# The opening of a hybrid trunk kernel and the step between its two passes, rewritten: stationary modulation blocks, other row statistics, input put in tile by tile

## The chip, the cores and the metric

One core of a Trainium2 chip runs the whole program. The metric is device time in microseconds, lower is better. PE is the matrix engine, PEld its weight loads, DVE the vector engine, ACT the scalar engine, POOL the third one, and SP issues nearly all DMAs from one queue in order.

## The reference, cut to what matters

One layer over 2048 latent tokens and 256 context tokens of width 1024, in float32. The token mixer is a bidirectional RG-LRU, a SwiGLU FFN follows. Both sub-layers begin with an RMS norm whose scale and shift come from a vector `c` (latent) or `c_ctx` (context):

```python
mx = split(silu(c) @ mod_w + mod_b, 6); mc = split(silu(c_ctx) @ mod_w + mod_b, 6)
hx = rms_norm(x, norm_mix_g) * (1 + mx[1]) + mx[0]       # 2048 tokens
hc = rms_norm(ctx, norm_mix_g) * (1 + mc[1]) + mc[0]     # 256 tokens
yx = rglru_mixer(hc, hx, ...)     # conv, gates, scans both ways, context first
x = x + mx[2] * yx
x = x + mx[5] * swiglu(modulate(rms_norm(x, norm_ffn_g), mx[3], mx[4]), ...)
```

So mx[0], mx[1], mc[0], mc[1] and the norm's row statistics (one 1/rms per token) have to stand before the first projection of the mixer, and the other four parts of mx not before the end of the mixer.

## The kernel before

Activations lie transposed: 128 channels on the partitions, tokens along the row; 1024 channels are eight tiles k. A float32 product is made of three float32r matmuls: `parts` (L83, L84) splits an operand into a rounded part (ACT copy) and its rest (DVE subtract), and `mm3` (L106 to L108) adds high by high, high by low and low by high. `norm` here means: a column of 1/rms values (`rstd_of`, fifteen small DVE instructions), spread over the partitions by a matmul of ones with a diagonal (`spread`, L138 and L142), copied out of PSUM by ACT.

**Sweep 1** covers the mixer's projections. The latent tokens stand in two halves s = 0 and s = 1 of 1024 tokens (two columns of 512 each), called the two passes here. Each pass runs over the ten 128-wide channel blocks n of the recurrence; m counts the 20 blocks. For each block `rec_unit` projects (48 matmuls of 512 columns; in pass 0 also 24 of 258 columns for the context), `conv` and `conv_parts` make the short convolution and split it, `gate_unit` projects the gate (48 matmuls of 512), `z_unit` makes the two gates of both directions (24 of 512; in pass 0 also 12 of 256 for the context), and `scan_exp`, `scan_root`, `scan_context`, `scan` finish the previous block. On PE, ACT and DVE the instructions of `blocks` stand in the order of the program text; SP's order is made by a scheduler. Weights come through `fetch`: a load into a buffer `raw` (4 of them), the split into a buffer `op` (6). Other buffers: `w` (9 rows of 1024), `hc` (4, the context's input), `hx` (8, the input of the pass at hand, so pass 1 takes over the buffers of pass 0), and four PSUM pairs of two banks.

**The opening** is everything ahead of the first `rec`. `first_loads` loads the context and the first 512 tokens; `mod_first` and four times `mod_quarter` make the scale A and shift B: the modulation weights are the moving operand, split like the others, 16 matmuls of 512 columns a quarter, with a stationary block that holds silu(c) and silu(c_ctx) in four columns; the result is turned back into a column by four narrow matmuls with `sel` (L256). `first_stats` squares all input tiles on ACT and sums over the channels with narrow matmuls (each tile's squares the stationary operand, one column of ones the moving one, L331): 56 for the context and the first 512 tokens, 32 for the second 512. `first_scale`, `first_apply` multiply by 1/rms, apply A and B and split. The order of the opening on all engines is the scheduler's. All of pass 0's input is ready before the first `rec`.

**The step between the passes** stands around blocks m = 8 and 9. `norm1_stats` has gathered sums of squares of the 1024 tokens of pass 1 from token-major rows (m = 0 to 7), `norm1_row` spreads 1/rms at m = 8, and then both remaining gates of pass 0 are projected, because they read `hx` for the last time; `norm1_apply` loads a tile of x (L379), scales it on DVE (L382), adds the shift and rounds on ACT (L383) and takes the rest on DVE (L384), for four tiles ahead of z(8), two ahead of z(9) and two behind it; rec(10) follows. The modulation's other 32 rows (`mod_rest`) are dot products on DVE, three for each block from m = 0 on.

Sweep 2 (the output projection and the FFN) starts when sweep 1 is done and isn't touched.

Of the kernel before, what the change touches and what calls it, by code (L numbers as in the profile page):

```python
# [44 lines left out]
class Trunk:  # L45
# [107 lines left out]
    def constants(self, first):  # L153
        nc, cp, io = self.nc, self.cp, self.io
# [4 lines left out]

        def load(key, shape):  # L160
            t = cp.tile(list(shape), F32, name=f"c_{key}")
            nc.sync.dma_start(t, io[key])
            return t

        cc = load("cc", (P, KD, 2))
        first()
        self.mod_b = load("mod_b", (P, 48))
        self.g_mix = load("g_mix", (P, KD))
        self.g_ffn = load("g_ffn", (P, KD))
# [5 lines left out]
    def constants_rest(self):  # L175
        nc, cp, io = self.nc, self.cp, self.io

        def load(key, shape):
            t = cp.tile(list(shape), F32, name=f"c_{key}")
            nc.sync.dma_start(t, io[key])  # L180
            return t

        self.conv_w = load("conv_w", (P, NB, 4))
        self.conv_b = load("conv_b", (P, NB))
        self.gate_b = load("gate_b", (P, 2, 2, NB))
        lam = load("lam", (P, 2 * NB))
        self.lam = lam
        self.state = cp.tile([P, 2, NB], F32, name="state")
        self.halo = cp.tile([P, NB, 4], F32, name="halo")

    def decay(self):
# [6 lines left out]
        self.behind(v.tensor_scalar(out=m, in0=lam, scalar1=-1.0, scalar2=0.0, op0=ALU.mult, op1=ALU.max),  # L198
                    self.scale_done)
        self.behind(v.tensor_scalar(out=e, in0=lam, scalar1=-1.0, scalar2=None, op0=ALU.mult), self.scale_done)  # L200
# [17 lines left out]
    def mod_first(self):  # L218

        nc = self.nc
        self.A = self.cp.tile([P, KD, 2], F32, name="A_mix")
        self.B = self.cp.tile([P, KD, 2], F32, name="B_mix")
        z = self.wp.tile([P, KD, P], F32, tag="raw", name="mod_z", bufs=RAWS)
        nc.gpsimd.memset(z, 0.0)
        st = self.wp.tile([P, KD, P], F32R, tag="op", name="mod_st", bufs=OPS)
        nc.vector.tensor_copy(z[:, :, 0:2], self.sc)  # L230
        nc.vector.tensor_copy(st, z)
        nc.vector.tensor_tensor(out=st[:, :, 2:4], in0=self.sc, in1=st[:, :, 0:2].bitcast(F32), op=ALU.subtract)
        sel = self.cp.tile([P, 2], F32, name="sel")
        nc.vector.tensor_tensor(out=sel, in0=self.ident[:, 0:2], in1=self.ident[:, 2:4], op=ALU.add)
        self.mod_st, self.sel = st, sel
        self.sc_row = self.te.tile([P, D], F32, tag="row", name="silu_row", bufs=1)
        for q in range(2):
            row = self.spread(self.sc[:, 4 * q : 4 * q + 4, 0], f"silu{q}")
            nc.vector.tensor_copy(self.sc_row[:, q * C : (q + 1) * C], row)

    def mod_quarter(self, q):
        nc, st, sel = self.nc, self.mod_st, self.sel
        ps = self.bank(f"ps_mod{q}")
        for j in range(KD // 2):
            raw = self.raw(self.io["mod_f"][q, j], f"modf{q}_{j}")
            self.last_mod = self.last_raw
            hl = self.parts(raw, f"modf{q}_{j}")
            for k in (2 * j, 2 * j + 1):
                for w in range(2):
                    nc.tensor.matmul(ps, st[:, k, :], hl[:, w, (k % 2) * C : (k % 2 + 1) * C],  # L250
                                     start=(k == w == 0), stop=(k == KD - 1 and w == 1))
# [37 lines left out]

    def norm1_stats(self, j):


        nc = self.nc
# [794 lines left out]
```

## Time and profile before

| | |
|---|---|
| three runs | 2366.94, 2371.41, 2372.65 us; median 2371.41 us |
| the profiled execution | 2367.48 us, of which the trace spans 2365.7 us |
| PE busy | 2236.8 us, 95% of the span |
| DVE, ACT busy | 1510.9 us (64%), 1170.9 us (49%) |
| mean granted clock of PE | 0.969 |

Matmuls are pipelined: a row's duration is longer than the distance to the next one, so distances of starts are used for rates. The granted clock is a share of 2.4 GHz; 0.5 is the lower of its two levels, 1.2 GHz. A line in brackets at the end of a row tells how long the engine was idle before it, and what ended that. Times of the trace are counted from the span's start.

### The profile page before, as it was taken

Reading aid. Unit: us, or ns where it says so; the run is one execution under the profiler, and the core shown is the slowest. Engines: PE = TensorE matmul, PEld = TensorE weight load, DVE = VectorE, ACT = ScalarE, POOL = GpSimd, SP = SyncE. Lnnn points to the kernel's source line nnn. Section 1 sums busy time; section 2 is a strip of 40 time slices with the busy share of each in tenths; the row PEclk is TensorE's granted clock in tenths of the full one; section 3 lists DMA queues with packets and bytes.
Section 4 is the critical chain, followed back from the end, with each engine's and each line's share of the span. In section 5 each row is a group of like instructions: output and inputs, shape, how many; then the busy total and the mean of one; then the engine's idle time right before and its main releaser. Section 6 shows DMA issues by size and latency. Waiting matters only on the chain.

```text
span 2365.7 us, 25944 instructions
## 1 busy us (share of the span) xinstructions
PE 2236.8 (95%) x9854; PEld 1844.2 (78%) x9854; DVE 1510.9 (64%) x1949; ACT 1170.9 (49%) x1416; POOL 1.6 (0%) x7
## 2 busy tenths in 40 slices
PE   7799997499999967999999999999999999999999
PEld 6688885388887855787877888878888888888887
DVE  5867776578888668767676555874555555545443
ACT  4467774577888325656564443453333333333332
POOL 0000000000000000000000000000000000000000
PEclk9699998799999988999999999999999999999999
DMA  6145453422123742444444476786522222246664
GB/s 227 64 160 178 169 178 112 164 80 67 63 74 105 276 143 89 143 151 142 152 144 145 161 238 221 219 289 229 188 81 81 80 80 81 80 134 211 226 220 144
DMA packets 127133, 354.14 MB, mean 150 GB/s; under 512 B 15136, under 2 KB 15136, under 8 KB 127008
## 3 DMA queue, kind: packets, MB, share of 16 engines
q1 hardware_dynamic: 127008, 352.48, 44.2%
q8 instruction: 77, 1.26, 0.2%
q14 instruction: 48, 0.39, 0.1%
HBM read 281.12 MB, written 71.30 MB: 149 GB/s over the span
## 4 chain that ended last, share of the span: by engine, by line
PE 67%; ACT 7%; DVE 4%; issue 2%; DMA 1%; DVEq 0%; ACTq 0%; SPq 0%
PE ps_dn L107 6%; PE ps_dn L108 6%; PE ps_dn L106 6%; PE ps_be L106 6%; PE ps_be L107 6%; PE ps_be L108 6%; PE ps_ep L108 3%; PE ps_wo L106 3%; PE ps_ep L107 3%; PE ps_wo L108 3%; PE ps_ep L106 3%; PE ps_wo L107 3%; ACT L77 2%; PE ps_rec L106 2%; PE ps_rec L107 2%
## 5 line engine op out<-in xcount | busy, mean ns | idle before, releaser
L107 PE MATMUL ps_dn<-op_xd,op_wd 128*128 128x512 f32 x704 | 274.2, 390 | 2.8 <-DVE op_xd L84 2.8
L108 PE MATMUL ps_dn<-op_xd,op_wd 128*128 128x512 f32 x704 | 273.9, 389 | 0.0
L106 PE MATMUL ps_dn<-op_xd,op_wd 128*128 128x512 f32 x704 | 269.9, 390 | 0.0
L84 DVE TENSOR_TENSOR op_wd<-raw_wd,op_wd 128x1024 fp32r<-128x1024 f32 x88 | 107.8, 1225 | 197.5 <-ACT op_wd L83 197.5
L83 ACT CAST op_wd<-raw_wd 128x1024 fp32r<-128x1024 f32 x88 | 92.7, 1054 | 265.9 <-PE ps_dn L108 214.6
L923 DVE TENSOR_TENSOR s<-ps_ep,s 128x512 f32<-128x512 f32 x88 | 60.7, 689 | 153.8 <-ACT s L948 114.6
L107 PEld LDWEIGHTS ps_dn<-op_xd,op_wd 128*128 128x128 f32 x704 | 132.1, 188 | 31.3 <-DVE op_xd L84 4.1
L106 PEld LDWEIGHTS ps_dn<-op_xd,op_wd 128*128 128x128 f32 x704 | 132.1, 188 | 28.0 <-ACT op_xd L83 0.4
L108 PEld LDWEIGHTS ps_dn<-op_xd,op_wd 128*128 128x128 f32 x704 | 132.1, 188 | 27.6
L106 PE MATMUL ps_be<-T,op_b 128*128 128x512 f32 x352 | 139.5, 396 | 9.5 <-ACT s L948 9.5
L77 ACT ACT_TABLE_LOAD x113 | 145.0, 1283 | 2.7 <-PEq L1082 0.7
L106 PE MATMUL ps_ep<-T,op_s 128*128 128x512 f32 x352 | 137.6, 393 | 8.3 <-ACT T L863 8.3
L108 PE MATMUL ps_be<-T,op_b 128*128 128x512 f32 x352 | 138.3, 393 | 0.0
L107 PE MATMUL ps_be<-T,op_b 128*128 128x512 f32 x352 | 138.3, 393 | 0.0
L108 PE MATMUL ps_ep<-T,op_s 128*128 128x512 f32 x352 | 137.4, 390 | 0.0
L107 PE MATMUL ps_ep<-T,op_s 128*128 128x512 f32 x352 | 137.2, 390 | 0.0
L106 PE MATMUL ps_rec<-hx,op_r 128*128 128x512 f32 x320 | 127.4, 398 | 7.5 <-ACT op_r L83 7.5
L948 ACT COPY s<-ps_be 128x512 f32<-128x512 f32 x44 | 25.7, 584 | 207.8 <-PE ps_be L108 207.8
L430 DVE SCALAR_TENSOR_TENSOR u<-ps_rec,c_conv_w,u 128x1024 f32<-128x1024 f32 x60 | 77.1, 1285 | 80.3 <-ACT u L427 78.8
L106 PE MATMUL ps_wo<-op_xo,op_wo 128*128 128x512 f32 x320 | 124.2, 393 | 2.6 <-ACT r L77 2.6
L107 PE MATMUL ps_rec<-hx,op_r 128*128 128x512 f32 x320 | 126.3, 395 | 0.2 <-DVE hx L357 0.2
L108 PE MATMUL ps_rec<-hx,op_r 128*128 128x512 f32 x320 | 126.1, 394 | 0.2 <-DVE op_r L84 0.2
(250 smaller groups left out, 5409.2 us busy)
## 6 DMA issues: line engine op xcount, KB each, us to landing
raw_wd<-in_down SPq DMA_DIRECT2D x88, 512.0 KB, 3.6
raw_xd<-d_act SPq DMA_DIRECT2D x88, 512.0 KB, 4.6
raw_ga<-in_gu SPq DMA_DIRECT2D x44, 512.0 KB, 3.9
raw_gb<-in_gu SPq DMA_DIRECT2D x44, 512.0 KB, 4.1
d_act<-s SPq DMA_DIRECT2D x88, 256.0 KB, 3.5
raw_xo<-d_rg SPq DMA_DIRECT2D x40, 512.0 KB, 4.2
raw_mod<-in_mod_t SPq DMA_DIRECT2D x32, 512.0 KB, 3.6
x<-in_x_t SPq DMA_DIRECT2D x48, 256.0 KB, 5.4
```

The source lines that it names most:

```text
L77: return self.table(self.nc.scalar.activation(out, in_, func, bias=bias, scale=scale))
L83: nc.scalar.copy(t[:, 0, :], raw)
L84: nc.vector.tensor_tensor(out=t[:, 1, :], in0=raw, in1=t[:, 0, :].bitcast(F32), op=ALU.subtract)
L106: ins = mm(ps, w[0], x[0], start=first, stop=False, skip_group_check=shared)
L107: mm(ps, w[0], x[1], start=False, stop=False, skip_group_check=shared)
L108: mm(ps, w[1], x[0], start=False, stop=last, skip_group_check=shared)
L430: v.scalar_tensor_tensor(out=part, in0=ps, scalar=cw[:, i : i + 1], in1=part, op0=ALU.mult, op1=ALU.add)
L923: v.tensor_tensor(out=t, in0=ps, in1=t, op=ALU.add)
L948: nc.scalar.copy(s3, be)
```

## The change

- **Modulation.** The weights are no longer split and no longer moving: each quarter is loaded as two tiles of 1 MB (`mod_load`), and `mod_half` takes each 128x128 block of it as the stationary operand, in float32, with the two columns silu(c), silu(c_ctx) as the moving one: 32 matmuls a quarter, 128 in all, into columns, so that no turning back is needed. Before, a float32 matmul of this kind appears in the trace as two instructions (two loads, two multiplications).
- **Statistics.** For the context and the first 512 tokens ACT squares and DVE adds over the tiles (`column_stats`), and seven narrow matmuls sum over the partitions; for the second 512 tokens the squares are summed along token-major rows on ACT (`token_stats`).
- **Input.** `apply` puts in a tile at a time: scale by A and 1/rms on DVE, shift and round on ACT, rest on DVE. The context's two extra columns are treated apart (`context_extra`).
- **Order.** The opening (`begin`) also stands in the order of the text on PE, ACT and DVE. Block 0's projections are taken into it and interleaved with the input: first half of rec and gate, context, second half of rec and gate. The decay constants are made at the start. `mod_rest` goes two and two for each block, none at m = 8, so that it is done before the step between the passes.
- **The step** (`turn`): the four first tiles of x are loaded into the `hc` buffers as soon as the context's input is no longer read, the diagonal is made at the head of m = 8, the spread follows rec(9) at once, and all eight tiles are put in behind the projection of gate(9); z(8), z(9) and rec(10) follow. `gate_unit` is cut into the projection and `gate_out` (the copy out of PSUM).

`mod_first`, `mod_quarter`, `norm1_stats`, `first_loads`, `first_stats`, `first_scale`, `first_apply`, `norm1_row` and `norm1_apply` go. The new code, with the unchanged and the removed lines left out where they tell nothing:

```diff
...
+    def mod_load(self, q):
+        ts = []
+        for half in range(2):
+            t = self.wp.tile([P, KD // 2, C], F32, tag="op", name=f"modf{q}_{half}", bufs=OPS)
+            self.nc.sync.dma_start(t, self.io["mod_f"][q, half])
+            ts.append(t)
+        return ts
+    def mod_half(self, ps, t, half):
+        for kk in range(KD // 2):
+            k = half * (KD // 2) + kk
+            for i in range(4):
+                self.nc.tensor.matmul(ps[:, i, :], t[:, kk, i * P : (i + 1) * P], self.sc[:, k, :],
+                                      start=(k == i == 0), stop=(k == KD - 1 and i == 3), skip_group_check=True)
...
+    def token_stats(self, t0, j, n, name):
+        nc = self.nc
+        xt = self.wp.tile([P, D], F32, tag="raw", name=f"xtok{name}{j}", bufs=RAWS)
+        nc.sync.dma_start(xt, self.io["x"][t0 + j * P : t0 + (j + 1) * P])
...
         nc.scalar.activation(xt, xt, AF.Square, accum_out=self.ss[:, j : j + 1])
+        return self.rstd_of(self.ss, f"rstd_{name}") if j == n - 1 else None
+    def column_stats(self, xs, n, name):
+        nc = self.nc
+        acc = self.wp.tile([P, S], F32, tag="raw", name=f"acc_{name}", bufs=RAWS)[:, :n]
+        for k, x in enumerate(xs):
+            if k == 0:
+                nc.scalar.activation(acc, x, AF.Square)
+            else:
+                sq = self.wp.tile([P, S], F32, tag="raw", name=f"sq_{name}{k}", bufs=RAWS)[:, :n]
+                nc.scalar.activation(sq, x, AF.Square)
+                nc.vector.tensor_tensor(out=acc, in0=acc, in1=sq, op=ALU.add)
+        return acc
+    def context_extra(self, xc, bc):
+        v = self.nc.vector
+        for h, t in enumerate(xc):
+            x = t[:, :, TC:]
+            ks = slice(4 * h, 4 * h + 4)
+            wide = lambda c: c[:, ks, 0:1].broadcast_to((P, 4, 2))
+            v.tensor_tensor(out=x, in0=x, in1=bc.unsqueeze(1).broadcast_to((P, 4, 2)), op=ALU.mult)
+            v.tensor_tensor(out=x, in0=x, in1=wide(self.A), op=ALU.mult)
+            v.tensor_tensor(out=x, in0=x, in1=wide(self.B), op=ALU.add)
+    def apply(self, x, bc, a, b, h, l):
+        v = self.nc.vector
+        v.scalar_tensor_tensor(out=x, in0=x, scalar=a, in1=bc, op0=ALU.mult, op1=ALU.mult)
+        self.nc.scalar.activation(h, x, AF.Identity, bias=b, scale=1.0)
+        v.scalar_tensor_tensor(out=l, in0=x, scalar=b, in1=h.bitcast(F32), op0=ALU.add, op1=ALU.subtract)
+    def apply_context(self, j, xc, bc):
+        nc = self.nc
+        t = self.hp.tile([P, 2, 2, TX], F32R, tag="hc", name=f"hc{j}", bufs=4)
+        for i in range(2):
+            k = 2 * j + i
+            self.apply(xc[:, k % 4, :TC], bc, self.A[:, k, 1:2], self.B[:, k, 1:2], t[:, i, 0, :TC], t[:, i, 1, :TC])
+        x = xc[:, 2 * j % 4 : 2 * j % 4 + 2, TC:]
+        nc.scalar.copy(t[:, :, 0, TC:], x)
+        nc.vector.tensor_tensor(out=t[:, :, 1, TC:], in0=x, in1=t[:, :, 0, TC:].bitcast(F32), op=ALU.subtract)
+        self.hc += [(t[:, i, 0, :], t[:, i, 1, :]) for i in range(2)]
...
+    def row_diag(self, y, name):
+        n = y.shape[-1]
+        t = self.wp.tile([P, S], F32, tag="raw", name=f"{name}_diag", bufs=RAWS)[:, : n * P]
+        self.nc.vector.tensor_tensor(
+            out=t.rearrange("p (n t) -> p n t", n=n), in0=self.ident.unsqueeze(1).broadcast_to((P, n, P)),
+            in1=y.unsqueeze(2).broadcast_to((P, n, P)), op=ALU.mult)
+        return t
+    def row_bc(self, diag, name):
+        n = diag.shape[-1]
+        row = self.te.tile([P, S], F32, tag="bc1", name=f"bc{name}", bufs=1)[:, :n]
+        ps = self.pair(f"{name}_bc")
+        for a in range(0, n, C):
+            self.nc.tensor.matmul(ps[:, a : a + C], self.ones, diag[:, a : a + C], start=True, stop=True)
+        self.nc.scalar.copy(row, ps[:, :n])
         return row
...
     def gate_unit(self, s, n, w):
...
         ps = self.pair(f"ps_gate{s}_{n}")
         self.project(s, ps, w)
+        return ps
+    def gate_out(self, s, n, ps):
+        nc = self.nc
...
+    def begin(self, blocks):
+        nc, io = self.nc, self.io
+        W = {}
+        self.constants()
+        mod = {0: self.mod_load(0)}
+        xc = []
+        for h in range(2):
+            t = self.te.tile([P, 4, TX], F32, tag="u", name=f"xc{h}", bufs=2)
+            nc.sync.dma_start(t, io["ctx_t"][:, 4 * h : 4 * h + 4, :])
+            xc.append(t)
+        mod[1] = self.mod_load(1)
+        x0 = [self.wtile(f"x0_{k}") for k in range(KD)]
+        for k in range(KD):
+            nc.sync.dma_start(x0[k][:, :C], io["x_t"][0][:, k, :C])
...
+        self.silu_row()
+        self.decay()
+        pm = {q: self.mod_bank(q) for q in range(2)}
+        for q in range(2):
+            for half in range(2):
+                self.mod_half(pm[q], mod[q][half], half)
+        mod[2] = self.mod_load(2)
+        acc = [self.column_stats([xc[k // 4][:, k % 4, :] for k in range(KD)], TX, "c"),
+               self.column_stats([x0[k][:, :C] for k in range(KD)], C, "x")]
+        mod[3] = self.mod_load(3)
+        for q in range(2):
+            self.mod_apply(q, pm[q])
+        ss = self.bank("ss_a")[:, :7]
+        for i, (a, t0) in enumerate([(0, 0), (0, P), (0, TX - P)] + [(1, j * P) for j in range(4)]):
+            nc.tensor.matmul(ss[:, i : i + 1], acc[a][:, t0 : t0 + P], self.ones[:, :1],
+                             start=(i == 0), stop=(i == 6), skip_group_check=True)
+        y = self.rstd_of(ss, "rstd_a")
+        pm = {q: self.mod_bank(q) for q in (2, 3)}
+        self.mod_half(pm[2], mod[2][0], 0)
+        bc0 = self.bc_sbuf(self.spread(y[:, 3:], "n1_0"), "n1_0")
+        bcc = self.bc_sbuf(self.spread(y[:, :3], "n1_c"), "n1_c")
+        self.mod_half(pm[2], mod[2][1], 1)
+        for half in range(2):
+            self.mod_half(pm[3], mod[3][half], half)
+        self.fetch(W, "r", blocks, 0)
+        self.constants_rest()
+        hx = self.hx[0] = self.hx_tiles(0)
+        a, b = (lambda k: self.A[:, k, 0:1]), (lambda k: self.B[:, k, 0:1])
+        first, second = slice(0, C), slice(C, S)
+        for k in range(KD):
+            if k == KD // 2:
+                for q in (2, 3):
+                    self.mod_apply(q, pm[q])
+            self.apply(x0[k][:, first], bc0, a(k), b(k), hx[k][0][:, first], hx[k][1][:, first])
+            if k >= KD // 2:
+                y = self.token_stats(C, k - KD // 2, 4, "b")
+        for k in range(KD):
+            nc.sync.dma_start(x0[k][:, second], io["x_t"][0][:, k, second])
+        self.fetch(W, "g", blocks, 0)
+        wr, wg = W.pop(("r", 0)), W.pop(("g", 0))
+        pr, pg = self.pair("ps_rec0_0"), self.pair("ps_gate0_0")
+        self.project(0, pr, wr, (0,))
+        diag = self.row_diag(y, "n1_1")
+        self.hc = []
+        self.context_extra(xc, bcc[:, 3 * P - 2 : 3 * P])
+        for j in range(KD // 2):
+            self.apply_context(j, xc[j // 2], bcc[:, :TC])
+            if j == 0:
+                self.project(0, pg, wg, (0,))
+                bc1 = self.row_bc(diag, "n1_1")
+        psc = self.pair("ps_recc_0")[:, :TX]
+        self.project(0, psc, wr, ctx=self.hc)
+        for k in range(KD):
+            self.apply(x0[k][:, second], bc1, a(k), b(k), hx[k][0][:, second], hx[k][1][:, second])
+        self.project(0, pr, wr, (1,))
+        self.project(0, pg, wg, (1,))
+        self.fetch(W, "r", blocks, 1)
+        U0 = self.conv(0, 0, pr, psc)
+        self.conv_parts(U0)
+        self.gate_out(0, 0, pg)
+        return W, U0
...
+        turn = NB - 2
...
+        def modulation(n):
+            for _ in range(n):
+                if rest:
+                    self.mod_rest(rest.pop(0))
...
         for m in range(M + 1):
             p = m - 1 if m > 0 else None
             fetch("z", m)
             fetch("r", m + 2)
...
+            if m == turn:
+                diag = self.row_diag(y, "n1_2")
+            else:
+                modulation(2)
             if p is not None:
                 self.scan_exp(U[p])
             if m + 1 < M and m + 1 != NB:
                 rec(m + 1)
+            if m == turn:
+                row = self.row_bc(diag, "n1_2")
+                xr = [self.hp.tile([P, S], F32, tag="hc", name=f"xr{k}", bufs=4) for k in range(4)]
+                for k in range(4):
+                    nc.sync.dma_start(xr[k], self.io["x_t"][1][:, k, :])
             if p is not None:
                 self.scan_root(U[p])
                 if U[p]["s"] == 0:
                     self.scan_context(U[p])
                 self.scan(U[p], 0)
+            if m != turn:
+                modulation(2)
             if m + 1 < M and m + 1 != NB:
                 self.conv_parts(U[m + 1])
             fetch("g", m + 1)
             if m < S // P:
...
+                y = self.token_stats(S, m, S // P, "n")
...
+            if m == turn:
+                self.turn(gate, m, blocks, row, xr)
                 z(m)
                 self.z_inputs(U[m])
...
+            elif m == turn + 1:
                 z(m)
...
                 self.z_inputs(U[m])
                 rec(m + 1)
                 self.conv_parts(U[m + 1])
             elif m < M:
...
+                if m > 0:
+                    self.gate_out(*blocks[m], gate(m))
                 z(m)
                 self.z_inputs(U[m])
+    def turn(self, gate, m, blocks, row, xr):
+        nc = self.nc
+        v = nc.vector
+        pg = gate(m)
+        for k in range(4, KD):
+            t = self.wtile(f"xr{k}")
+            nc.sync.dma_start(t, self.io["x_t"][1][:, k, :])
+            xr.append(t)
+        scale = lambda k: v.scalar_tensor_tensor(
+            out=xr[k], in0=xr[k], scalar=self.A[:, k, 0:1], in1=row, op0=ALU.mult, op1=ALU.mult)
+        for k in range(4):
+            scale(k)
+        self.gate_out(*blocks[m], pg)
+        pg = gate(m + 1)
+        hx = self.hx[1] = self.hx_tiles(1)
+        for k in range(KD):
+            h, l = hx[k]
+            b = self.B[:, k, 0:1]
+            nc.scalar.activation(h, xr[k], AF.Identity, bias=b, scale=1.0)
+            v.scalar_tensor_tensor(out=l, in0=xr[k], scalar=b, in1=h.bitcast(F32), op0=ALU.add, op1=ALU.subtract)
+            if k + 4 < KD:
+                scale(k + 4)
+        self.gate_out(*blocks[m + 1], pg)
```

## Rows read from the trace of the kernel before

**Rows 1.** The page, busy time, share of the span and instructions of each engine.

```profile
PE 2236.8 (95%) x9854; PEld 1844.2 (78%) x9854; DVE 1510.9 (64%) x1949; ACT 1170.9 (49%) x1416; POOL 1.6 (0%) x7
```

**Rows 2.** Windows: length, busy PE, PEld, DVE, ACT, POOL (instructions), PEclk, DMA share, GB/s.

```profile
140.00:371.00 231.00, 231.00 (x1142) 196.30 (x1141) 180.76 (x265) 169.81 (x218) 0.00 (x0) 1.00 0.49 172
378.60:473.30 94.70, 46.56 (x173) 35.54 (x173) 49.57 (x55) 39.61 (x47) 0.00 (x0) 0.71 0.32 114
500.00:720.00 220.00, 220.00 (x972) 182.23 (x971) 176.34 (x157) 175.08 (x164) 0.00 (x0) 1.00 0.20 65
```

**Rows 3.** Waits of PE in 84 to 760: total us, times, longest.

```profile
PE ps_z L106 <- ACT rc L77: 28.6, 2, 18.0
PE n_bc L142 <- DVE n_diag L138: 21.6, 3, 16.9
PE ps_rec L106 <- ACT op_r L83: 7.5, 1, 7.5
```

**Rows 4.** Timeline of PE, narrow matmuls of the opening: start, us, what.

```profile
8.94 23.89 PE L331 MATMUL ss_a<-ones,sqa 128*128 128x1 f32 x112
...
39.21 1.05 PE L256 MATMUL ps_modc<-sel,mod_rows 128*128 128x2 f32 x8 [0.71 <-ACT mod_rows L253]
...
66.81 13.18 PE L331 MATMUL ss_b<-ones,sqb 128*128 128x1 f32 x64
```

**Rows 5.** Groups by line, 0 to 110: busy us, mean ns, idle before.

```profile
L331 PE MATMUL ss_a<-ones,sqa 128*128 128x1 f32 x112 | 23.9, 351 | 0.0
...
L250 PE MATMUL ps_mod<-op_modf,mod_st 128*128 128x512 f32 x64 | 20.3, 482 | 0.0
...
L130 DVE TENSOR_TENSOR rstd_b_y<-rstd_b_y,rstd_b_q 128x4 f32<-128x4 f32 x3 | 0.5, 162 | 0.1
```

**Rows 6.** Windows of the opening, columns as in the second group.

```profile
66.80:67.80 1.00, 1.00 (x10) 1.00 (x9) 1.00 (x5) 0.39 (x2) 0.00 (x0) 0.85 0.07 20
67.80:80.00 12.20, 12.20 (x58) 12.11 (x57) 8.21 (x23) 5.17 (x11) 0.00 (x0) 0.50 0.00 0
9.00:12.00 3.00, 3.00 (x17) 3.00 (x15) 0.69 (x1) 1.48 (x3) 0.00 (x0) 1.00 1.04 385
```

**Rows 7.** Timelines around the step: DVE's gate weights, PE's spread, SP's loads.

```profile
393.57 1.22 DVE L84 TENSOR_TENSOR op_g<-raw_g,op_g 128x1024 fp32r<-128x1024 f32 x1
...
395.54 2.05 PE L142 MATMUL n_bc<-n_diag,ones 128*128 128x512 f32 x2 [16.87 <-DVE n_diag L138]
...
413.65 2.26 SPq L379 DMA_DIRECT2D xr<-in_x_t  x4
```

**Rows 8.** Timeline of DVE and ACT, input of pass 1.

```profile
418.75 1.29 DVE L382 SCALAR_TENSOR_TENSOR xr<-xr,A_mix,bcn 128x1024 f32<-128x1024 f32 x1 [20.44 <-DMA xr<-in_x_t]
...
426.41 1.28 DVE L382 SCALAR_TENSOR_TENSOR xr<-xr,A_mix,bcn 128x1024 f32<-128x1024 f32 x1
...
427.73 1.15 ACT L383 ACTIVATE hx<-xr,B_mix 128x1024 fp32r<-128x1024 f32 x1 [2.55 <-DVE xr L382]
...
430.11 1.28 DVE L382 SCALAR_TENSOR_TENSOR xr<-xr,A_mix,bcn 128x1024 f32<-128x1024 f32 x1
```

**Rows 9.** Groups by line, 860 to 925 in sweep 2, same operations 512 wide.

```profile
L854 DVE SCALAR_TENSOR_TENSOR x1n<-x1n,A_ffn,bcn 128x512 f32<-128x512 f32 x16 | 11.3, 746 | 5.6 <-ACT bcn L148 5.6
...
L866 ACT ACTIVATE T<-x1n,modv 128x512 fp32r<-128x512 f32 x12 | 7.9, 715 | 2.3 <-DVE x1n L854 2.3
```

**Rows 10.** Timeline of PE, second rec and first gate.

```profile
108.79 0.80 PE L106 MATMUL ps_rec<-hx,op_r 128*128 128x512 f32 x1 [7.52 <-ACT op_r L83]
...
126.08 0.39 PE L106 MATMUL ps_gate<-hx,op_g 128*128 128x512 f32 x1
...
136.73 0.39 PE L108 MATMUL ps_gate<-hx,op_g 128*128 128x512 f32 x1
```

**Rows 11.** Timeline of ACT, from z(8)'s gates to the next weights.

```profile
436.29 1.28 ACT L77 ACT_TABLE_LOAD   x1
...
443.24 0.61 ACT L83 CAST op_z<-raw_z 128x512 fp32r<-128x512 f32 x1
...
444.81 1.28 ACT L77 ACT_TABLE_LOAD   x1
...
453.12 1.03 ACT L83 CAST op_g<-raw_g 128x1024 fp32r<-128x1024 f32 x1
```

More of the change, by code (lines that the diff above doesn't have):

```diff
@@ L149, in bc_sbuf, with load, constants @@
         return bc
-    def constants(self, first):
-        nc, cp, io = self.nc, self.cp, self.io
+    def load(self, key, shape):
+        t = self.cp.tile(list(shape), F32, name=f"c_{key}")
+        self.nc.sync.dma_start(t, self.io[key])
+        return t
+    def constants(self):
+        nc, cp = self.nc, self.cp
         self.ident = cp.tile([P, P], F32, name="ident")
@@ L158, in constants @@
         nc.vector.memset(self.ones, 1.0)
[L160 to L169, printed above, removed]
+        cc = self.load("cc", (P, KD, 2))
+        self.mod_b = self.load("mod_b", (P, 48))
+        self.g_mix = self.load("g_mix", (P, KD))
+        self.lam = self.load("lam", (P, 2 * NB))
         self.sc = cp.tile([P, KD, 2], F32, name="silu_c")
@@ L216, in decay, with silu_row @@
         v.tensor_scalar_mul(self.c_t.rearrange("p d n -> p (d n)"), p, 0.5 * LRU_C)
[L218 to L235, printed above, removed]
+    def silu_row(self):
         self.sc_row = self.te.tile([P, D], F32, tag="row", name="silu_row", bufs=1)
@@ L238, in mod_first, with mod_bank, mod_apply @@
             row = self.spread(self.sc[:, 4 * q : 4 * q + 4, 0], f"silu{q}")
[L239 to L251, printed above, removed]
-        rows = self.tp.tile([P, S], F32, tag="w", name=f"mod_rows{q}", bufs=WS)
-        nc.scalar.copy(rows[:, :C], ps)
-        pc = self.bank(f"ps_modc{q}")[:, :8].rearrange("p (i s) -> p i s", s=2)
-        for i in range(4):
-            mm = nc.tensor.matmul(pc[:, i, :], rows[:, i * P : (i + 1) * P], sel,
-                                  start=(i == 0), stop=(i == 3), skip_group_check=True)
-        self.mod_done = mm.ins.name
+            self.nc.vector.tensor_copy(self.sc_row[:, q * C : (q + 1) * C], row)
+    def mod_load(self, q):
[11 more added lines that the diff above has]
+                                      start=(k == i == 0), stop=(k == KD - 1 and i == 3), skip_group_check=True)
+    def mod_bank(self, q):
+        return self.bank(f"ps_mod{q}")[:, :8].rearrange("p (i s) -> p i s", s=2)
+    def mod_apply(self, q, pc):
+        v = self.nc.vector
         kb, part = (q // 2) * 4, q % 2
@@ L666, in gate @@
         def gate(m):
[L667 removed]
+            return self.gate_unit(*blocks[m], W.pop(("g", m)))
         def z(m):
             self.z_unit(U[m], W.pop(("z", m)))
[L672 to L676 removed]
         for m in range(M + 1):
```

194 lines of the change are left out of this document (28 added, 166 removed).

## Prediction

> **What bounds the kernel now.** The page comes first: PE is busy for 95% of the span, DVE for 64%, ACT for 49% [rows 1]. A busy PE can only be helped where it idles or runs at its lower clock, so the second view is the table of windows over sweep 1. In pass 0 from 140 to 371 and in pass 1 from 500 to 720 PE is busy without a gap at full clock, while DVE has 180.8 of 231 and ACT 169.8 of 231 us; in between, from 378.6 to 473.3, PE has 46.6 busy us of 94.7 at a mean clock of 0.71 [rows 2]. The third view, PE's waits, names what ends the gaps: twice the input of pass 1 (z's matmuls wait for PSUM that ACT empties, 28.6 us in two waits, because ACT is held by the input tiles), the diagonals of the norm's spread (21.6 us in three), and the weights of block 1 (7.5 us, at the end of the opening) [rows 3]. The reader is to see that sweep 1 loses time in two places only, the opening and the step, that both are in the change, and that each is a chain over DVE, ACT and PE whose length is a sum.
>
> **The opening.** What the old path did on PE goes whole, the narrow matmuls of the statistics (23.9 and 13.2 us) [rows 4] and the 64 wide ones of the modulation (20.3 us) [rows 5]. I therefore don't subtract, but time the new path from its start to the end of gate(0) and compare it with the old one.
>
> A narrow float32 matmul is two instructions. In `ss_a` 112 of them took 23.89 us, 0.213 each; with two columns and at the higher clock eight took 1.05, 0.131 each [rows 4]. Which of the two holds? In `ss_b` the clock was still mostly high in the first us (0.85) and then 0.50 for 12.2 us in which PE was busy without a gap, 58 instructions at 0.210 [rows 6]. So a gapless stream of narrow matmuls let the clock fall and did not bring it back, and the 0.213 of `ss_a` is the same low rate (the window there shows 1.00 at its head, but the distances are those of 0.50). I take 0.213: the modulation's 128 matmuls are 256 instructions, 54.6 us (33.5 at 0.131).
>
> Two sections of one page of the Trainium skill, "TensorE: Matmul & The Clock Gate", bear on it, and neither enters the sum. Section "LDWEIGHTS (loading the stationary operand)", puts a load at the number of columns over 1.2, 107 ns for 128 columns whatever the rows: an estimate of 27.3 us for 256 loads, and a total some 27 us below mine; the trace shows 131 to 213 ns for a load with its matmul. Section "Part 1: The HAM clock gate" says that sustained matmul activity releases the throttle; by that rule the stream would run at the high rate, and the trace of `ss_b` does not agree.
>
> The chain, in us from the start. The narrow stream begins at 9.0 as `ss_a` did, behind the two spreads of silu [rows 4]. Quarters 0 and 1: 128 instructions, 27.3, to 36.3. Their 4 MB and the 3 MB of input are there by then, since the loads ran at 385 GB/s [rows 6]. The squares on ACT, the sums on DVE and the decay constants lie beside this stream. Seven matmuls of the statistics: 3.0, to 39.3; half of quarter 2: 6.8, to 46.1 (the rstd, fifteen times 0.2 on DVE [rows 5], beside it); two spreads at the low clock, one of 2.05 [rows 7], one of three quarters of that, and a diagonal between them: 4.4, to 50.5; 96 more instructions: 20.4, to 70.9. Tiles 0 to 3 of the first 512 tokens and the split of the first weights are done meanwhile. Then A and B for tiles 4 to 7: 0.7, to 71.6.
>
> Now DVE and ACT set the pace. `apply` is DVE, ACT, DVE in order, and DVE can't start the next tile while it waits for ACT. For 1024 columns one tile takes 430.11 less 426.41, 3.70 us, which is the sum of its three durations [rows 8]. For 512 the durations are 0.746, 0.715 and 0.746 [rows 9], 2.2 a tile. Tiles 4 to 7: 8.8, to 80.4. The last square and rstd of the second 512 tokens, 3.4, and the split of gate(0)'s weights behind it on DVE, 1.2: 85.0. Only then can PE begin gate(0)'s first half; rec(0)'s ended at about 81. Matmuls of 512 columns come every (136.73 - 126.08)/47 = 0.227 us [rows 10]; 24 take 5.4, and after a stop more: rec(1) took 17.3 us from 108.79 to 126.08 [rows 10] against 48 x 0.227 and 24 of half that, 13.7, so a restart costs up to 3.6. With 3.0: 93.4. The spread of the second row, 2.05, and its copy, 0.6: 96.0. That copy stands in ACT's queue ahead of three of the four pairs of context tiles, and DVE's next tiles wait behind them: six tiles of 256 columns at 1.45 (estimate: 3.70, 2.2 and the line through both) and small pieces, 9, to 105.0. Eight tiles of the second half: 17.6, to 122.6. PE follows tile by tile; last tile 0.7, second half of gate(0) 5.4 and 2.6 for the clock: 131. There rec(0) and gate(0) are done and rec(1) remains, 13.7: 144.7. The old kernel had all three at 137.0 [rows 10]. **The opening loses 8**; if PE keeps its clock in both restarts, 2; if the context tiles wait longer, 13.
>
> **Pass 0.** PE has no gap there and keeps none: `mod_rest` does four dot products a block for eight blocks in place of three, 1.2 us more on DVE, which has 50 us in 231 free [rows 2]. The cost is nothing; without that cover it would be 8 x 1.2 = 10. In return the blocks of the step have no dot products.
>
> **The step.** Zero is the end of rec(9) at 378.6 [rows 2]. The old chain: the diagonals stood behind everything on DVE, so the spread began at 395.5 after 16.9 us of idle PE [rows 7]; the loads of x stood behind the store of gate(8) in SP's queue, and DVE waited 20.4 us for the first until 418.75 [rows 7, 8]; then eight tiles at 3.70 with z(8) and z(9) caught between them, and rec(10) at 94.7.
>
> The new chain. The diagonal stands at the head of m = 8, so two spreads follow rec(9) at once: 2.2 at full clock. Gate(8): 10.9, to 13.1. Gate(9) needs its weights' split, which keeps its place in DVE's queue: 393.57 + 1.22 - 378.6 = 16.2 [rows 7]; to 27.1. From 16.2 on DVE has sixteen scalings and rests of 1.28 with nothing to wait for, since four scalings run ahead of ACT: 20.5, to 36.7. ACT ends its last tile 1.3 us after the last scaling (31.5), at 32.8; gate(9)'s copy 1.0: 33.8. z(8)'s table and gates: 443.24 - 436.29 = 6.95, to 40.8; two weight splits 1.6; the previous block's exp and root 453.12 - 444.81 = 8.3, to 50.7 [rows 11]; the next split, z(9)'s table load and its four short gates (1.0 + 1.3 + 1.4), 54.4; they free the PSUM pair for z(9)'s last product, which takes 1.4 to 2.6: rec(10) starts at 56. With a restart of 3.6, of which the old kernel had paid most before its 94.7, it counts as 59.5. **The step gains 35.** Bounds: PE's own work alone is 2.2 + 21.8 + 13.7 = 37.7, a gain of at most 57; if the new `hx` tiles can't be written before gate(9) has read its last one (27.1), all moves by 7 and the gain is 28. x's first four tiles are loaded into the context's buffers, which rec(9)'s context part gives back some 5 us before zero, so they are there at 16.2; tiles 4 to 7 queue behind the forward scan's store on SP, at about 13, and are needed from 21 on.
>
> **Sum.** +8 - 35 = -27 on the profiled 2367.5 us: 2340.5. The median of the runs is 3.9 above that execution and the mean of all four 2.1; I add about 2: **2342**.
>
> **Rivals.**
> 1. The narrow stream runs at the high rate, because PE is busy without a gap. 256 and 14 instructions at 0.131 take 22 less, and everything behind them moves up: 2320. For it: two columns at 0.131 [rows 4]. Against: the clock fell in `ss_b` while PE was busy [rows 6]. Chance 0.10. It is the case that the Trainium skill's Part 1 on the clock gate describes.
> 2. The loads of x are as late as before. If the scheduler leaves them behind gate(8)'s store, the first scaling comes not at 16.2 but after gate(8)'s end, the copy and a landing of 5.1 (418.75 - 413.65), at about 20, and tiles 4 to 7 later still; if they then wait for each store, as in the old kernel, 40 [rows 7, 8]. The step gains 11 and the total is 2366, no change. For it: SP's order is the scheduler's. Against: the loads stand well ahead of the stores in the text. Chance 0.07.
> 3. Slower: load and matmul of the narrow pairs don't overlap, because each matmul needs a fresh block of another tile. Then an instruction costs its full duration, 0.351 [rows 5], 256 make 90 us instead of 55, the opening loses 43 and the total is 2377. It decides from 0.32 on. For it: nothing but the new operands; against: `ss_a` too has a new block each time and does 0.213 [rows 4]. Chance 0.06.
>
> **How the numbers follow.** My forecast has 0.74, the rivals 0.23, the rest is open to both sides. The forecast's own range: opening +2 to +13, step -28 to -40, so 2330 to 2356. The range over all takes in rival 1 and leaves out rivals 2 and 3: 2320 to 2357. A change within 0.3% (7 us) can't be told from none. Faster 0.86, same 0.08, slower 0.06.
>
> **What would show it.** Narrow matmuls at 0.21 a piece in two blocks of some 27 us with a clock of 0.50; gate(0) of block 0 ending near 131 and block 1's rec behind it; tiles at 2.2 us; no wait of PE for x between 380 and 440; rec(10) some 56 us behind rec(9). Wrong would be: a narrow rate of 0.13 or 0.35, a gap in pass 0 that DVE ends, or a scaling that waits for a load.

## The result, and the profile after

The kernel before took 2370.9 us in the runs beside it, the changed one 2342.9 (median of four, 2341.7 to 2345.9): a ratio of 0.9886, 95% interval 0.9869 to 0.9903, so 28 us or 1.1% faster. The forecast was 2342. The profiled execution took 2343.9 (span 2342.2).

First the page's busy line, then windows of the changed kernel (columns as in [rows 2]): the opening's second half, pass 0, the step from the end of rec(9) to the start of rec(10), pass 1.

```profile
PE 2253.5 (96%) x9852; PEld 1852.4 (79%) x9852; DVE 1489.7 (64%) x1912; ACT 1156.4 (49%) x1399; POOL 0.7 (0%) x6
...
71.20:127.60 56.40, 46.74 (x123) 29.00 (x123) 36.94 (x80) 22.07 (x39) 0.00 (x0) 0.70 0.16 52
...
160.00:350.00 190.00, 190.00 (x944) 161.62 (x943) 153.88 (x223) 138.62 (x178) 0.00 (x0) 1.00 0.55 190
388.90:445.10 56.20, 43.49 (x174) 33.69 (x173) 45.96 (x48) 41.61 (x48) 0.00 (x0) 0.90 0.33 122
500.00:720.00 220.00, 217.92 (x962) 180.13 (x961) 179.86 (x154) 176.34 (x164) 0.00 (x0) 1.00 0.22 72
```

The reader sees that the step is 56.2 us long where it had 94.7 [rows 2], and that pass 0 still has no gap. PE's longest waits from 0 to 760 (total us, times, longest) have become short:

```profile
PE ps_z L106 <- ACT rc L77: 8.0, 3, 5.3
PE ps_gate L108 <- DVE op_g L84: 5.5, 2, 3.1
...
PE ps_recc L106 <- ACT hc L317: 4.0, 3, 1.9
...
PE ps_z L106 <- DVE u L407: 2.5, 1, 2.5
```

Against [rows 3], the 28.6 for ACT's gates is 8.0, and the 21.6 for the diagonals is gone. The step in PE's and DVE's timelines (start, us):

```profile
388.91 1.88 PE L340 MATMUL n_bc<-n_diag,ones 128*128 128x512 f32 x4
405.24 0.50 PE L108 MATMUL ps_gate<-hx,op_g 128*128 128x512 f32 x1 [3.08 <-DVE op_g L84]
...
442.33 0.79 PE L106 MATMUL ps_z<-uhl,op_z 128*128 128x512 f32 x1 [5.33 <-ACT rc L77]
...
445.06 0.63 PE L106 MATMUL ps_rec<-hx,op_r 128*128 128x512 f32 x1
...
403.97 1.22 DVE L84 TENSOR_TENSOR op_g<-raw_g,op_g 128x1024 fp32r<-128x1024 f32 x1
405.11 4.87 DVE L740 SCALAR_TENSOR_TENSOR xr<-xr,A_mix,bcn 128x1024 f32<-128x1024 f32 x4
409.89 1.28 DVE L751 SCALAR_TENSOR_TENSOR hx<-xr,B_mix,hx 128x1024 fp32r<-128x1024 f32 x1
...
419.46 4.87 DVE L751 SCALAR_TENSOR_TENSOR hx<-xr,B_mix,hx 128x1024 fp32r<-128x1024 f32 x4
```

The spread follows rec(9) at once, the first scaling starts 16.2 after it, no scaling or rest waits for anything, and rec(10) starts 56.2 after it. The opening went as follows:

```profile
9.27 27.31 PE L228 MATMUL ps_mod<-silu_c,modf 128*128 128x2 f32 x128
...
143.76 0.39 PE L108 MATMUL ps_z<-uhl,op_z 128*128 128x512 f32 x1
146.70 0.47 PE L106 MATMUL ps_z<-uhl,op_z 128*128 128x512 f32 x1 [2.55 <-DVE u L407]
...
147.24 0.63 PE L108 MATMUL ps_z<-uhl,op_z 128*128 128x512 f32 x1
147.67 0.63 PE L106 MATMUL ps_z<-uhl,op_z 128*128 128x512 f32 x1
...
152.74 0.50 PE L106 MATMUL ps_z<-uhl,op_z 128*128 128x512 f32 x1 [1.45 <-ACT rc L77]
...
154.24 0.39 PE L106 MATMUL ps_rec<-hx,op_r 128*128 128x512 f32 x1
```

128 narrow instructions in 27.31 are 0.213 each. rec(0), gate(0) and rec(1) are done at 141.2 (before: 137.0). Then z(0) waits 2.55 and 1.45, and behind the first wait its matmuls come 0.43 apart instead of 0.23: rec(2) starts at 154.24, where the kernel before had it at 143.85. That is 10.4 later, and rec(9) ends 10.3 later, at 388.9. So up to the start of sweep 2: 10.3 lost, 37.5 to 38.5 gained, 27.2 net (first `ps_wo` at 721.6 instead of 748.8).

One caution on single traces: the same code doesn't take the same time in every execution. In the six kernels that share this opening up to gate(0), gate(0) ends between 126.4 and 128.5; from rec(11)'s end to the first `ps_wo` it takes between 253.5 and 258.4; and in sweep 2, the same code in all kernels here, between 702.8 and 708.8 from the first `ps_wo` to the first `ps_dn`. The 3.7 by which the profiled span of the changed kernel falls short of the net gain (23.5 against 27.2) came in there and behind it. Below, positions are therefore read in sweep 1, small differences as distances inside one trace, and times from medians.

### The profile page after: what moved, and what is told of

It is laid out like the page before. It is cut to its first block, busy times and chain, and to the rows that moved or that the text cites. A ratio compares the mean times of both kernels' runs of the same rounds, so it can differ in the third digit from the quotient of the medians.

```text
span 2342.2 us, 25844 instructions
## 1 busy us (share of the span) xinstructions
PE 2253.5 (96%) x9852; PEld 1852.4 (79%) x9852; DVE 1489.7 (64%) x1912; ACT 1156.4 (49%) x1399; POOL 0.7 (0%) x6
## 4 chain that ended last, share of the span: by engine, by line
PE 68%; ACT 7%; DVE 3%; issue 2%; DMA 1%; SPq 0%; DVEq 0%; ACTq 0%
PE ps_dn L107 6%; PE ps_dn L108 6%; PE ps_dn L106 6%; PE ps_be L106 6%; PE ps_be L107 6%; PE ps_be L108 6%; PE ps_ep L108 3%; PE ps_ep L107 3%; PE ps_ep L106 3%; PE ps_wo L106 3%; PE ps_wo L107 3%; PE ps_wo L108 3%; ACT L77 2%; PE ps_rec L108 2%; PE ps_rec L107 2%
## 5 line engine op out<-in xcount | busy, mean ns | idle before, releaser
L108 PE MATMUL ps_gate<-hx,op_g 128*128 128x512 f32 x320 | 127.0, 397 | 5.5 <-DVE op_g L84 5.5
L106 PE MATMUL ps_rec<-hx,op_r 128*128 128x512 f32 x320 | 129.6, 405 | 2.1 <-ACT hx L306 2.1
L107 PE MATMUL ps_rec<-hx,op_r 128*128 128x512 f32 x320 | 129.4, 404 | 0.6 <-DVE hx L307 0.6
L108 PE MATMUL ps_rec<-hx,op_r 128*128 128x512 f32 x320 | 127.7, 399 | 0.0
```

The costliest lines, as they stand in the source:

```text
L106: ins = mm(ps, w[0], x[0], start=first, stop=False, skip_group_check=shared)
L107: mm(ps, w[0], x[1], start=False, stop=False, skip_group_check=shared)
L108: mm(ps, w[1], x[0], start=False, stop=last, skip_group_check=shared)
```

## The experiments

Theory: the step alone gains about 38, the opening alone loses about 10, and they add. Rivals: the new opening is part of the gain; or the parts depend on each other.

**Each half by itself.** The old opening with the new `turn` and four dot products a block, and the new opening with the old `norm1_apply` and three.

> The opening of the kernel before with the step of the changed kernel (four dot products a block, the diagonals at the head of block 8, x loaded early, scalings ahead of ACT). Theory (the step gains about 38, the opening loses about 10): the step alone is worth 2370.9 - 37.5 = 2333, some 10 below the changed kernel; rec(10) starts about 56 us after rec(9) ends. Rival (the gain needs the new opening, which frees DVE or the queues): between 2343 and 2371.

> The opening of the changed kernel with the step of the kernel before (three dot products a block, also in block 8, diagonals late, x's loads behind gate(8)'s store). Theory: slower than the kernel before by the 10 that the opening loses, 2381 (2376 to 2386). Rival (the new opening is no loss, or is part of the gain): 2371 or less.

Measured: 2328.5 (ratio 0.9832, interval 0.9819 to 0.9846) and 2382.0 (1.0056, 1.0043 to 1.0068), beside 2369.1 for the kernel before. That is -40.6 and +12.9; their sum, -27.7, agrees with the change's -28.0. The first came 4.5 under its forecast of 2333: up to the first `ps_wo` its trace gains 37.3 (711.5 against 748.8), as forecast, and the rest lies in sweep 2 (703.8 against 707.7). Windows of the old opening with the new step:

```profile
137.15:142.80 5.65, 5.65 (x27) 4.69 (x26) 1.92 (x2) 5.64 (x8) 0.00 (x0) 1.00 0.58 219
377.30:433.40 56.10, 43.18 (x173) 33.69 (x172) 45.88 (x48) 41.54 (x48) 0.00 (x0) 0.89 0.33 122
```

The step is 56.1 long with either opening, and z(0) at 137.15 has no wait and the full rate, although its block has the same four dot products: they aren't what stalls z(0) in the changed kernel. In the new opening with the old step PE's waits from 380 to 500 are those of before:

```profile
PE ps_z L106 <- ACT rc L77: 29.8, 2, 19.2
PE n_bc L142 <- DVE n_diag L138: 17.7, 2, 16.9
```

**What in the step gains.** Three kernels each undo one of its parts.

```diff
-                diag = self.row_diag(y, "n1_2")
...
             if m < S // P:
                 y = self.token_stats(S, m, S // P, "n")
+            if m == turn:
+                row = self.row_bc(self.row_diag(y, "n1_2"), "n1_2")
```

> The changed kernel with the diagonals of the step's row put back behind the scans and the weight splits of block 8, where the kernel before had them; all else as changed. Theory (the step is one chain, DVE to PE to ACT to DVE): the spread starts about 17 after rec(9) ends, as before; gate(8) no longer covers that time, gate(9) ends near 41 in place of 29, ACT's input tiles can't go into the hx buffers before gate(9) has read them, and rec(10) comes some 12 to 15 later: 2355 to 2358. Rival (the wait is covered by the scans, z and the loads): 2343.

```diff
         pg = gate(m)
+        store = self.gate_out(*blocks[m], pg)
...
+            self.behind(nc.sync.dma_start(xr[k], self.io["x_t"][1][:, k, :]), store)
```

> The changed kernel with the eight loads of pass 1's input behind the store of gate(8) in SP's queue. The prediction's rival 2 priced this, with a wait for each store, at 23, a total of 2366. Theory now: only the first tile is late, gate(8)'s end 13.3 after rec(9), its copy 1.0 and a landing of 5.1 make 19.5 to 20.5 where the scalings now start at 16.2, and the others follow faster than DVE's 2.56 a tile: 4 to 6 more, 2347 to 2349.

```diff
-        for k in range(4):
-            scale(k)
...
+            scale(k)
             nc.scalar.activation(h, xr[k], AF.Identity, bias=b, scale=1.0)
...
-            if k + 4 < KD:
-                scale(k + 4)
```

> The changed kernel with the step's scalings no longer four ahead of ACT: each tile goes DVE, ACT, DVE in order, as in the kernel before; diagonals and loads stay early. Theory: a tile takes 3.70 instead of 2.56, so the last rest ends 9 to 12 later, the copy of gate(9), the sigmoids of z(8) and z(9) and rec(10) with it: 2352 to 2355. Rival (ACT's input tiles wait for gate(9)'s reading anyway, so the lead of the scalings is worth little): 2343 to 2347.

Measured, with the distance from the end of rec(9) to the start of rec(10) in the trace:

| kernel | us | ratio (interval) | step |
|---|---|---|---|
| before | 2369.3 | 1 | 94.7 |
| changed | 2342.9 | 0.9886 (0.9869 to 0.9903) | 56.2 |
| diagonals late | 2354.2 | 0.9933 (0.9921 to 0.9946) | 70.0 |
| loads late | 2347.4 | 0.9909 (0.9896 to 0.9923) | 61.4 |
| scalings not ahead | 2354.5 | 0.9938 (0.9923 to 0.9952) | 69.4 |

Each ratio is to the runs of the kernel before beside it, whose medians lie between 2369.1 and 2370.9. Diagonals 11, loads 5, order of the scalings 12. The intervals of the loads and of the changed kernel overlap, so the 5 rests on the step: 61.4, where every other kernel here with the new step unaltered has 56.1 to 56.2. The diagonals came in just under the expected range, the other two inside it. Together the three make 28 of the 38 to 41 that the step gains; what the rest comes from (the new places of z(8) and z(9), the dot products gone from m = 8, parts that cover for each other) no run separates. Three excerpts, one of each kernel's trace, show the mechanism. PE's wait with late diagonals:

```profile
PE n_bc L340 <- DVE n_diag L329: 17.4, 1, 17.4
```

DVE's first scaling with late loads, 20.0 behind the end of rec(9) (389.44) instead of 16.2:

```profile
409.47 1.28 DVE L739 SCALAR_TENSOR_TENSOR xr<-xr,A_mix,bcn 128x1024 f32<-128x1024 f32 x1 [3.75 <-DMA xr<-in_x_t]
```

DVE with the scalings not ahead, a tile each 3.77, of which 1.28 is a wait for ACT:

```profile
408.01 1.28 DVE L740 SCALAR_TENSOR_TENSOR xr<-xr,A_mix,bcn 128x1024 f32<-128x1024 f32 x1
410.58 1.28 DVE L750 SCALAR_TENSOR_TENSOR hx<-xr,B_mix,hx 128x1024 fp32r<-128x1024 f32 x1 [1.28 <-ACT hx L749]
411.78 1.28 DVE L740 SCALAR_TENSOR_TENSOR xr<-xr,A_mix,bcn 128x1024 f32<-128x1024 f32 x1
```

**Is 0.213 a matter of the clock?** Wide matmuls of constants were mixed into the narrow stream, one to four narrow ones and then one to one.

```diff
             for i in range(4):
                 self.nc.tensor.matmul(ps[:, i, :], t[:, kk, i * P : (i + 1) * P], self.sc[:, k, :], ...)
+            self.nc.tensor.matmul(self.wide, self.warm, self.warm.unsqueeze(1).broadcast_to((P, 4, P)), ...)
```

> The changed kernel with one 512-column float32r matmul of constants, into an unused half of the PSUM pair, behind every fourth narrow matmul of the opening (32 in all; their result is not read). If the narrow stream runs at 0.213 a piece because narrow matmuls don't hold the clock up, the wide ones raise it: the stream's 256 instructions go to 0.131 and take 21 less, the wide ones cost 32 x 0.23 = 7; the first block may then wait for loads, so 6 to 14 less: 2329 to 2337. If 0.213 is the price of a narrow pair at any clock, the wide ones only add 7 to 14: 2350 to 2357.

> As the run with one wide matmul to four narrow ones, but with one 512-column matmul of constants behind each narrow matmul (128 in all, results not read). With one to four a wide one took 0.427 at the low rate and a narrow instruction 0.213. If the narrow rate hangs on the clock and this much wide work raises it, the wide ones come down to about 0.227 and the narrow pair to 2 x 0.131 at the same place: the stream takes 128 x 0.49 = 63, and the kernel some 8 more than the changed one, 2351. If the clock rises and the narrow pair stays at 0.213, 84: 2372. If the clock stays low, 109: 2397.

Measured: 2355.1 (0.9946, 0.9934 to 0.9959), and 2396.7 in a single run. PE's timeline with one to one, at the end of the stream:

```profile
123.88 0.42 PE L230 MATMUL ps_mod<-silu_c,modf 128*128 128x2 f32 x2
124.16 0.77 PE L232 MATMUL ps_mod<-warm 128*128 128x512 f32 x1
124.74 0.42 PE L230 MATMUL ps_mod<-silu_c,modf 128*128 128x2 f32 x2
125.02 0.77 PE L232 MATMUL ps_mod<-warm 128*128 128x512 f32 x1
125.59 0.63 PE L106 MATMUL ps_rec<-hx,op_r 128*128 128x512 f32 x1
126.02 0.63 PE L107 MATMUL ps_rec<-hx,op_r 128*128 128x512 f32 x1
...
128.65 0.39 PE L108 MATMUL ps_rec<-hx,op_r 128*128 128x512 f32 x1
128.88 0.39 PE L106 MATMUL ps_rec<-hx,op_r 128*128 128x512 f32 x1
```

rec(0) starts at 125.59 where the changed kernel has it at 70.74, 54.9 later for 128 wide ones: 0.43 each, which is also the distance of rec's matmuls at 126, 512 columns at 1.2 GHz, the low level. The other 0.43 of the 0.86 for a pair and a wide one is the pair, 0.213 an instruction. A few matmuls on, in rec alone, the distance is 0.23, the high level. So the stream runs at the low level to its last instruction, PE busy almost without a gap since 9.3, and the mixed-in matmuls only add their own time. Both times are near forecasts in which the wide ones only add (2350 to 2357, and 2397); but the first of these gave as reason that 0.213 is the price at any clock, and that is not so.

That the low level is why a narrow instruction takes 0.213 is shown by the kernel before. In its `ss_b`, one stream without a gap, seven instructions start from 66.81 to 67.48, 0.112 apart; from there on they are 0.213 apart, and the recorded clock falls at that place. The first row is from PE's timeline up to 67.5, the other two are windows of this stream alone (length, PE, PEld, DVE, then clock, DMA share, GB/s):

```profile
66.81 1.02 PE L331 MATMUL ss_b<-ones,sqb 128*128 128x1 f32 x7
...
66.80:67.50 0.70, 0.69 (x7) 0.70 (x7) 0.00 (x0) 1.00 0.10 29
67.50:80.00 12.50, 12.49 (x60) 12.41 (x59) 0.00 (x0) 0.50 0.00 0
```

What the modulation's whole stream would take at the high level isn't shown: no stream of its length ran there. The page's granted clock reads 1.00 all through the stream, but it prints 1.00 wherever the trace holds no clock record, and in the changed kernel the first record is at 75.5, where rec's matmuls go from 0.43 to 0.23 apart. Ahead of it the level has to be read from distances of wide matmuls. By the Trainium skill, page "TensorE: Matmul & The Clock Gate", section "Part 1: The HAM clock gate", sustained matmul activity would have released the throttle; this trace does not agree for a stream with narrow float32 matmuls in it.

**What sets the opening's second half.** First only the order of the step's scalings, brought to the opening's `apply`. Then, besides, what needs only quarters 0 and 1 moved ahead, where DVE and ACT stand idle under the narrow stream.

```diff
+        scale(*items[0])
+        for j, (x, bc, a, b, h, l) in enumerate(items):
+            self.nc.scalar.activation(h, x, AF.Identity, bias=b, scale=1.0)
+            if j + 1 < len(items):
+                scale(*items[j + 1])
+            v.scalar_tensor_tensor(out=l, in0=x, scalar=b, in1=h.bitcast(F32), op0=ALU.add, op1=ALU.subtract)
```

> The changed kernel with the opening's apply in the order of the step's: the scaling of tile k+1 stands on DVE ahead of the rest of tile k, so DVE doesn't wait for ACT. Theory (the chain DVE, ACT, DVE sets the pace of the opening's second half): 2.20 a tile becomes 1.46, four tiles of the first half give 3, the context 2 to 3, eight of the second half 6: 8 to 11 less, 2332 to 2335. Rival (PE's restarts at the low clock, or the stall of z(0), take it back): 0 to 3 less.

```diff
+        self.apply_many([item(k, bc0, first) for k in low])
+        for j in range(4):
+            y = self.token_stats(C, j, 4, "b")
+        self.fetch(W, "r", blocks, 0)
...
+        self.fetch(W, "g", blocks, 0)
...
+        self.apply_context(hc, xc, bcc[:, :TC], low)
+        diag = self.row_diag(y, "n1_1")
         for q in (2, 3):
             self.mod_apply(q, pm[q])
```

> The changed kernel with scalings ahead of ACT in the opening (as in the earlier run) and, besides, with what needs only quarters 0 and 1 moved under the narrow stream, where DVE and ACT stand idle: context tiles 0 to 3, the token statistics and the row of the second 512 tokens, and the loads of x's second half and of gate(0)'s weights ahead. Theory (behind 71 us the chain over DVE sets the pace of the opening): the pipelined version ends gate(0) at 113.8; here four tiles of the first half, four of the context and eight of the second remain, 6 + 4.5 + 12, and gate(0) ends near 101: 13 less than 2330.3, 2317. Rival (PE's own work at the low clock sets the pace from 71 on: 24 + 24 + 48 matmuls of 512 columns at up to 0.36 and the context's 24): at most 6 less, 2325 to 2330.

Measured: 2330.3 (0.9840, 0.9826 to 0.9853) and 2316.8 (0.9770, 0.9756 to 0.9785), the first a little better than the theory's range, the second at its number. gate(0) ends at 113.8 and 100.1 instead of 127.6. The window from rec(0)'s start to gate(0)'s end, with the work moved ahead:

```profile
71.90:100.10 28.20, 28.11 (x123) 22.60 (x122) 25.52 (x46) 14.13 (x23) 0.00 (x0) 1.00 0.12 38
```

The same 123 records keep PE busy for 28.1 us here and for 46.7 in the changed kernel, where the clock reads 0.70. The chain over DVE costs twice: in gaps of PE, and in the low level that PE runs at behind them. (The 1.00 of this window is recorded from 76.8 on only; before that rec's matmuls come 0.43 apart here too.)

**The stall of z(0).** z(0) stands right behind rec(1) on PE, since gate(0) moved into the opening. Here z(0) goes ahead of rec(1), first in the changed kernel, then with the work moved ahead.

```diff
+        z(0)
+        self.z_inputs(U[0])
+        fetch("r", 1)
         for m in range(M + 1):
```

> The changed kernel with z(0) ahead of rec(1) on PE, ACT and DVE (after gate(0), and its weights split ahead of conv(0)). Theory (z(0) pays 6 more than its own 7 because it stands right behind rec(1): four PSUM pairs taken, ACT behind conv(1)): now z(0) waits only for its own input, some 2 to 3 after gate(0), and rec(1) follows without a gap: 3 to 4 less, 2339. Rival (the stall comes from the dot products or the clock at m = 0, and only moves): 2343.

> The version with the work moved under the narrow stream and z(0) ahead of rec(1): if the two are independent, the sum of both, 2317 - 3.5 = 2313; if z(0)'s wait for its own input grows since nothing hides conv(0) any more, the same as without: 2317.

Measured: 2341.9 (0.9883, 0.9866 to 0.9899), which can't be told from the changed kernel, and 2314.9 (0.9760, 0.9745 to 0.9775), between the two forecasts and within the interval of 2316.8. By the time the rival's 2343 was nearer, and the trace bears it out. In the first kernel z(0) has no wait; rec(1) has one instead, for its weights' split behind the sigmoids on ACT:

```profile
135.53 0.80 PE L106 MATMUL ps_rec<-hx,op_r 128*128 128x512 f32 x1 [2.14 <-ACT op_r L83]
...
151.20 0.39 PE L106 MATMUL ps_rec<-hx,op_r 128*128 128x512 f32 x1
```

rec(2) starts at 151.2, 3.0 earlier; but gate(0), whose code is the same, had already ended 1.2 earlier in this execution (126.4 against 127.6), so the move is worth 1.9 there, not 3 to 4. z(1) then waits 1.2 that it did not wait before, and from gate(0)'s end to rec(9)'s end it takes 261.2 here and 261.4 in the changed kernel: the wait has moved, and next to nothing is gained. With the work moved ahead the same distance goes from 264.3 to 261.8. The waits of the changed kernel say what holds z(0) there, conv(1) and then ACT, and the dot products are out by the old opening's z(0). That PE's order alone costs the 6 is not shown, since this order doesn't bring them home; how much another could stays open.

**A miss.** The modulation alone put back to wide matmuls with split weights, behind the statistics.

> The changed kernel with one part undone: the four modulation quarters by 64 wide float32r matmuls with split weights, as in the kernel before, behind the new statistics (which now come first); apply, tile order and step as changed. Theory (the narrow stream of 54.6 us, to 71, holds the opening, and the chain of apply follows it): the quarters end with their loads, 8 MB at 385 GB/s, and with 16 splits of 1.05 on ACT and 1.23 on DVE, at about 42 to 45; then eight tiles at 2.20 in place of four, 62 where the changed kernel has 80.4: 18 less, 2325. Rival (the splits on DVE, which the stationary blocks save, cost as much as the narrow stream): 2335 to 2345.

Measured: 2348.9 (0.9920, 0.9907 to 0.9934), slower than either forecast. Its PE waits from 9 to 80, and a window, say why:

```profile
PE ss_a L606 <- DVE acc_c L301: 11.1, 1, 11.1
...
PE ps_mod L233 <- DVE op_modf L84: 3.7, 4, 1.2
...
30.00:40.00 10.00, 5.41 (x7) 2.09 (x8) 4.42 (x10) 4.21 (x6) 0.00 (x0) 1.00 0.19 71
```

The first wide matmul came at 37.9 and the last quarter ended at 72.5, not 45. The splits need the four `raw` buffers that the squares use too, so from 30 to 40 the loads moved 71 GB/s, and then a quarter took 7.5 to 9 us at 240 to 270 GB/s instead of 385. I take the buffers for the cause, without a run that shows it. This tells that my order was bad and not what the splits would cost in a good one.

## Why the prediction was right, step by step

- **Narrow stream**: 0.213 a piece, quarters 0 and 1 from 9.0 to 36.3, the rest to 70.9. Measured 9.27 to 36.57 and 70.88. Rivals 1 (0.131) and 3 (0.35) are out. The estimate from the Trainium skill, page "TensorE: Matmul & The Clock Gate", section "LDWEIGHTS (loading the stationary operand)", 27.3 for all 256 loads, is what the first 128 alone took, at the low level. Two details of the prediction don't hold. Its sign "a clock of 0.50" did not show: the page reads 1.00 there, for want of a record. And its 0.131 divides 1.05 by eight, but the 1.05 contains the last instruction's own 0.25; the starts are 0.112 apart, so rival 1 would have meant about 2315 and not 2320. Neither changes the sum.
- **Chain of apply**: 2.2 a tile, measured 2.20. gate(0)'s first half was put at 85.0 to 93.4 and ran from 84.7 (two matmuls stood ahead of the wait for the split) to 92.1; gate(0)'s end was put at 131 and came at 127.6, because the last tile was done at 119.6 and not at 122.6. The opening loses 4 up to rec(1)'s end, not 8.
- **What was missing**: z(0). The sum ended with rec(1) and took for granted that block 0 goes on as before. In the kernel before gate(0) stood between rec(1) and z(0), 11 us in which conv(1) gave back its PSUM pairs and ACT came to the sigmoids; with gate(0) moved ahead z(0) took 6 more. So "the opening loses 8", which measured 10.3, was itself 3.5 too much up to rec(1) and 6 too little behind it.
- **Pass 0**: no gap with four dot products, as said.
- **Step**: rec(10) 56 behind rec(9), measured 56.2. The gain was put at 35, after a charge of 3.6 for PE's restart, and measured 38.5 at rec(10)'s start and 37.5 at rec(11)'s end: the charge came out at 1.0, since rec(10) took 12.1 us where the old kernel took 11.1. The first scaling at 16.2 and gate(9)'s copy behind the last input tile (33.8 predicted, ended at 32.8) were where the sum had them.
- **Rival 2** asked for late loads, 2366. They were early; made late, they cost 4.5, not 23. Its price held the old kernel's wait for each store, which the new order doesn't have.
- The terms were off by +2.3 (opening) and -2.5 (step), so part of the agreement, 2342 against 2342.9, is luck: errors cancelled between the two halves and inside the opening.

The best order tried is the changed kernel with the early work and z(0) ahead: 2314.9, 2.4% under the kernel before and 1.2% under the changed one (without the move of z(0) 2316.8, which can't be told from it). The old opening with the new step, 2328.5, also beats both.

## What to carry to other kernels

Time a rewritten stretch to the point where the schedules are the same again, not to the last unit that was rewritten: a unit moved forward takes away the cover of the one that stood behind it. In a chain DVE, ACT, DVE let the first step run a tile ahead; here that was worth 12 us twice. A long stream that only PE can work on is a cover: see what DVE and ACT could already do under it.

## What the runs showed of the hardware

- Narrow float32 instructions started 0.112 apart at the high level and 0.213 apart at the low one, in one stream of the kernel before; the clock fell at 67.5 while PE was busy with them.
- With a 512-column float32r matmul to each narrow float32 one TensorE stayed at its low level from the first to the last of that stream (9.3 to 125.6); rec's matmuls alone, right behind it, rose to the high one.
- The granted clock of the page read 1.00 over all of that stream, while wide matmuls came 0.43 apart: the trace has no clock record there. Later, between stops of PE, the page did show the fall (0.50 from 104 to 121 in the changed kernel).
- Profiled executions of kernels that share sweep 2 differed by up to 6 us in its first part (702.8 to 708.8).
